# Two-layer decoder trunk: x given with its features on partitions, 1/rms applied where the projections are evicted, layer B's first weights made in the output projection's last chunk

## The chip, the cores and the metric

One NeuronCore of a Trainium2 chip. The time is the device time of one execution in microseconds (us), the median of several runs. TensorE is PE (its weight loads PEld), VectorE DVE, ScalarE ACT, GpSimd POOL; SP issues nearly all DMAs, in the order of its own queue.

## The reference

Two decoder layers over x of 2048 tokens (S) and 1024 features (D), in fp32. Cut to what matters here:

```python
def rmsnorm(x, g):
    return x * rsqrt(mean(x * x, -1) + EPS) * g
# layer A: 16 heads of 64
u = rmsnorm(x, norm_a_g)
q, k, v, f, gate = split(u @ w_in_a)
q, k = rmsnorm(q, qnorm_a_g), rmsnorm(k, knorm_a_g)          # per head
o = causal_attention(q, k, v, bias=cumsum(log_sigmoid(f + b_forget)))
h = x + (o * silu(gate)) @ w_out_a
# keys and values of layer B, and layer B
k_s, v_s = split(rmsnorm(h, kv_norm_g) @ w_kv)                # k: norm, rope
q, gate = split(rmsnorm(h, norm_b_g) @ w_in_b)                # q: norm, rope
o = sliding_window_attention(q, k_s, v_s, sinks)
out = h + (o * silu(gate)) @ w_out_b
```

## The kernel before

Every fp32 operand of a large matmul is kept as two fp32r parts, high and low, and a product is three matmuls (high by high, high by low, low by high). A projection of 128 tokens onto 512 columns takes 8 pieces of 128 features, so 24 matmuls of 512 columns. "Block" is 128 tokens (16 of them, NTB), "chunk" 512 tokens (4, CH).

The stages in order of time, with lines of the kernel before:

- **Layer A's projections**, 12 to 604 us, `projections` (matmul L586): seven groups of columns, each over 16 blocks; the first is a group of v heads. In the first group `normer.upto` loads a block of x with tokens on partitions (L308, into tiles st and wr in turn), takes its squares' sum on ACT (L310), its 1/rms with small DVE operations and one ACT square root (L296 to L301), multiplies the block by it (DVE L314), turns it with eight PE transposes into a PSUM buffer b2 (L287), and splits that into the high part (ACT L323) and the low part (DVE L324). These parts (tiles big) stay for the other groups, and are written out for the gate.
- **Attention of layer A**, 605 to 1473 us: scores L803 and L804, values L844, running sums L829. The gate projection (L875; 32 tiles of 128 features by 512 tokens, 24 matmuls each, one PSUM buffer pb) is fed in between, matmul by matmul, by `feed`; 28 tiles fall into this stage. A finished gate tile goes through ACT (Tanh, L882) and DVE (L883).
- **Output projection of layer A**, 1500 to 1683 us, `out_a` (L1071): per chunk eight tiles of 128 tokens by 512 columns. Each loads its part of x into a buffer qn (L1061), adds it to PSUM (L1075) and stores h from the same buffer (L1076). Beside a chunk the gated inputs of the next are made (`gated`, L1027 to L1031, loads into st and wr). In the last chunk, which has no next one, layer B's norm of the first blocks runs: loads of h, transposes, splits.
- **Layer B's projections**, 1683 to 1990 us, the same `projections`: the first group's weights are w_kv, in four loads of 512 KB through two buffers wr (L349), and each is split into two wh (ACT L366) and two wl (DVE L367).
- **Gate of layer B** to 2180 us (L557, Silu L563), and attention and output projection of layer B to the end.

Order: each engine runs its instructions in one fixed order, which a scheduler makes from the program; buffers come round in turn, so that an operation waits until the last reader of its buffer is done. b2 has three PSUM buffers, shared by projections, transposes and out_a; pa and pb one each. SBUF buffers: wr 2, st 4, qn 3, wh and wl 9 each, big 8.

Of the kernel before, what the change touches and what calls it, by code (L numbers as in the profile page):

```python
# [13 lines left out]
F32R = mybir.dt.float32r  # L14
# [8 lines left out]
P = 128  # L23
# [31 lines left out]

JOBS_AT = (0, 3, 6, 9)
# [17 lines left out]
SLOTS = dict(big=8, st=4, wr=2, wh=9, wl=9, sq=2, qn=3, rot=1, ro1=1, ro2=2)  # L74
# [13 lines left out]
class Trunk:  # L88
# [7 lines left out]
    def __init__(self, ctx, tc, a, out):  # L96
# [4 lines left out]
            for name, shape in (  # L101
# [9 lines left out]
                ("rd", [H, S]),  # L111
                ("h1", [S, D]),
# [176 lines left out]
    def rstd(self, sm, n, count):  # L289
# [5 lines left out]
        ss, v, r, t = (sm[:, i, :n] for i in range(4))  # L295
# [5 lines left out]
        nc.vector.scalar_tensor_tensor(r, t, 1.5, r, ALU.add, ALU.mult)  # L301
        return r

    def norm(self, src, tb, junk):

        nc = self.nc
        xt = self.sb(("st", "wr")[tb % 2], [P, D])
        nc.sync.dma_start(out=xt, in_=src[tb * P : (tb + 1) * P, :])  # L308
        sm = self.sb("sm", [P, 4, 8], bufs=4)
        nc.scalar.activation(  # L310
            junk, xt.rearrange("p (c t) -> p c t", t=P), AF.Square, accum_out=sm[:, 0, :1]
        )
        r = self.rstd(sm, 1, D)
        nc.vector.tensor_scalar(xt, xt, r, None, ALU.mult)  # L314
        return xt

    def norm_transpose(self, xt, uh, ul):

        nc = self.nc
        ps = self.ps("b2", [P, NDT, P])  # L320
        for dt in range(NDT):
            self.flip(ps[:, dt, :], xt[:, dt * P : (dt + 1) * P])
        nc.scalar.copy(uh, ps)  # L323
        nc.vector.tensor_tensor(ul, ps, f_(uh), ALU.subtract)  # L324
# [49 lines left out]
    def qk_norm(self, ps, nh, tb, rope):  # L374
# [4 lines left out]
        nc.scalar.activation(sq, pv, AF.Square)  # L379
        sm = self.sb("sm", [P, 4, 8], bufs=4)  # L380
        nc.vector.tensor_reduce(sm[:, 0, :nh], sq, AX.X, ALU.add)  # L381
        r = self.rstd(sm, nh, HD)
        qn = self.sb("qn", [P, nh, HD])
# [36 lines left out]
    def v_tile(self, ps, nh, dst):  # L420
        nc = self.nc
        st = self.sb("sq" if nh <= 4 else "st", [P, nh, P])
        pv = ps.rearrange("p (h d) -> p h d", d=HD)
        nc.scalar.copy(r_(st[:, :, :HD]), pv)
        nc.vector.tensor_tensor(r_(st[:, :, HD:]), pv, st[:, :, :HD], ALU.subtract)  # L425
        nc.sync.dma_start(out=dst, in_=st)

# [10 lines left out]
    def normer(self, src):  # L438

        uh, ul, ready = {}, {}, []  # L440
# [8 lines left out]

        def upto(n, loads=()):  # L450

            while done[1] < min(n, NTB):
                while done[0] < min(done[1] + LOADED_AHEAD, NTB):
                    _, junk = parts(done[0])
# [920 lines left out]
```

## Time and profile before

| | |
|---|---|
| median of 3 runs | 2541.59 us (2537.08 to 2541.75) |
| the profiled execution | 2537.57 us, its span 2535.7 us |
| mean granted TensorE clock | 0.996 |
| TensorE busy | 2477.2 us (98% of the span) |
| VectorE, ScalarE, GpSimd busy | 67%, 53%, 37% |

The profile is of one execution; all times inside it are from its span's start. TensorE's idle time is short and scattered, but for the start, the end of the attention and the join of the layers near 1684 us.

### The profile page before, as it was taken

What the parts mean: (1) busy time and instruction counts of PE and PEld (TensorE: products, weight loads), DVE (VectorE), ACT (ScalarE), POOL (GpSimd) and SP (SyncE); (2) the same over time, 40 slices, a digit from 0 to 9 for tenths busy, and PEclk for the clock granted to TensorE, in tenths of its full rate; (3) what the DMA queues carried; (4) which work ended last, traced back from release to release, by engine and by line L of the source; (5) the groups of instructions that cost most, each with busy time, mean ns of one, the idle gap of its engine ahead of it and who ended that gap; (6) DMA issues with size and microseconds to landing.
All of it is one profiled execution on the core that took longest, in us unless ns stands there. A gap on an engine that the chain in (4) does not pass through costs nothing.

```text
span 2535.7 us, 37563 instructions
## 1 busy us (share of the span) xinstructions
PE 2477.2 (98%) x12414; PEld 2065.3 (81%) x12414; DVE 1693.9 (67%) x4158; ACT 1335.0 (53%) x2614; POOL 941.3 (37%) x611
## 2 busy tenths in 40 slices
PE   8999999999999999999999999989999999899999
PEld 7888899987878787877887778767888888788887
DVE  5555556636888888888888964437666301788885
ACT  5423323314777787877787731124332213777774
POOL 0000000013777777877788832200011000355552
PEclk9999999999999999999999999999999999999999
DMA  5656555686545655565456678935434424756651
GB/s 185 181 153 188 163 148 170 186 272 207 158 143 138 188 159 151 158 180 151 126 152 200 178 232 264 274 127 150 125 108 109 143 82 127 196 156 162 169 143 66
DMA packets 355217, 416.13 MB, mean 164 GB/s; under 512 B 65072, under 2 KB 248368, under 8 KB 348848
## 3 DMA queue, kind: packets, MB, share of 16 engines
q1 hardware_dynamic: 355024, 413.75, 56.5%
q8 instruction: 98, 1.61, 0.3%
q14 instruction: 95, 0.78, 0.1%
HBM read 262.13 MB, written 151.39 MB: 163 GB/s over the span
## 4 chain that ended last, share of the span: by engine, by line
PE 84%; DMA 7%; DVE 4%; ACT 2%; issue 2%; SPq 1%; POOL 1%; DVEq 0%; ACTq 0%; POOLq 0%
PE b L586 30%; PE pa L844 9%; PE b L557 7%; PE pb L1217 6%; PE pb L875 6%; PE sc L803 5%; PE mx L755 5%; PE sc L804 5%; PE b L287 3%; DMA wr<-rd 3%; PE b L1071 2%; PE pa L1182 2%; PE b L1126 1%; PE b L1123 1%; PE pb L287 1%
## 5 line engine op out<-in xcount | busy, mean ns | idle before, releaser
L586 PE MATMUL b<-wh,big 128*128 128x512 f32 (+3 forms) x2560 | 774.3, 376 | 11.7 <-ACT wh L366 7.9
L818 POOL TENSOR_TENSOR big<-st,big 128x1024 fp32r<-128x1024 f32 (+1 forms) x320 | 680.6, 2140 | 243.1 <-ACT big L817 163.7
L586 PEld LDWEIGHTS b<-wh,big 128*128 128x128 f32 x2560 | 473.4, 189 | 83.4 <-ACT wh L366 10.4
L586 PE MATMUL b<-wl,big 128*128 128x512 f32 (+3 forms) x1280 | 475.8, 372 | 0.3 <-DVE wl L367 0.3
L829 DVE TENSOR_TENSOR ac<-ac,st 128x512 f32<-128x512 f32 (+3 forms) x576 | 355.0, 616 | 60.4 <-ACT ac L821 23.1
L844 PE MATMUL pa<-big 128*128 128x512 f32 (+2 forms) x1280 | 332.6, 373 | 3.0 <-POOL big L818 2.0
L812 ACT ACTIVATE st<-sc 128x512 f32<-128x512 f32 (+1 forms) x512 | 275.3, 584 | 103.5 <-PE sc L804 67.8
L817 ACT CAST big<-st 128x1024 fp32r<-128x1024 f32 (+1 forms) x320 | 302.2, 944 | 9.4 <-PE pa L844 1.2
L586 PEld LDWEIGHTS b<-wl,big 128*128 128x128 f32 x1280 | 242.8, 190 | 37.4 <-DVE wl L367 4.2
L844 PEld LDWEIGHTS pa<-big 128*128 128x128 f32 x1280 | 225.5, 190 | 43.6 <-ACT sq L852 7.4
L803 PE MATMUL sc<-big 128*128 128x512 f32 (+2 forms) x640 | 245.8, 384 | 1.4 <-DVE st L425 1.4
L766 DVE CUSTOM_DVE_ANT_0 mx<-mx,rot 128x128 f32<-128x128 f32 (+3 forms) x240 | 211.0, 879 | 44.7 <-PE mx L755 42.0
L804 PE MATMUL sc<-big 67*128 67x512 f32 (+2 forms) x640 | 236.2, 369 | 0.0
L379 ACT ACTIVATE sq<-b 128x512 f32<-128x512 f32 (+2 forms) x128 | 66.3, 518 | 322.2 <-PE b L586 321.1
L755 PE MATMUL mx<-big 66*128 66x128 f32 (+3 forms) x660 | 190.1, 361 | 2.6 <-DVE mt L766 1.5
L381 DVE TENSOR_REDUCE sm<-sq 128x8 f32<-128x512 f32 (+2 forms) x128 | 74.9, 585 | 162.0 <-ACT sq L379 161.6
L1071 PE MATMUL b<-big 128*128 128x512 f32 x768 | 177.6, 391 | 2.9 <-DVE qn L1075 1.8
L875 PE MATMUL pb<-wh,wr 128*128 128x512 f32 x448 | 166.2, 401 | 7.1 <-DMA wr<-wg 5.2
L1071 PEld LDWEIGHTS b<-big 128*128 128x128 f32 x768 | 143.1, 188 | 36.0 <-DVE qn L1075 3.9
L681 POOL MEMSET rot<- 128x1024 bf16 x1 | 1.0, 951 | 430.6 <-PE pb L287 430.6
L557 PE MATMUL b<-big,wh 128*128 128x512 f32 x512 | 158.7, 391 | 1.5 <-ACT st L563 1.5
L1152 POOL TENSOR_TENSOR st<-st,rs 128x1024 f32<-128x1024 f32 (+1 forms) x64 | 118.7, 1855 | 102.0 <-DVE rs L1151 87.8
(222 smaller groups left out, 4207.7 us busy)
## 6 DMA issues: line engine op xcount, KB each, us to landing
wr<-wg SPq DMA_DIRECT2D x60, 512.0 KB, 5.3
va<-st SPq DMA_DIRECT2D x32, 512.0 KB, 3.6
ka<-st SPq DMA_DIRECT2D x64, 256.0 KB, 3.8
ut<-big SPq DMA_DIRECT2D x16, 1024.0 KB, 5.5
big<-ka SPq DMA_DIRECT2D x16, 1024.0 KB, 6.5
big<-qa SPq DMA_DIRECT2D x16, 1024.0 KB, 5.0
qb<-st SPq DMA_DIRECT2D x64, 256.0 KB, 3.8
big<-qb SPq DMA_DIRECT2D x16, 1024.0 KB, 6.4
```

What stands on the lines that cost most here:

```text
L557: nc.tensor.matmul(ps, W[k][dt][:, ft * P : (ft + 1) * P], u[ch][:, dt, :], start=(dt == 0 and i == 0), stop=(dt == NDT - 1 and i == 2),)
L586: nc.tensor.matmul(ps[:, :n], u[tb // 4][:, dt, us], W[k][dt], start=(dt == 0 and i == 0), stop=(dt == NDT - 1 and i == 2),)
L755: mm = nc.tensor.matmul(ps[:, b, :wb], qb[:66, i * P : (i + 1) * P], kb[:66, k0 + b * wb : k0 + (b + 1) * wb], start=True, stop=True,)
L803: nc.tensor.matmul(o, ka[:, ks], qa[:, qs], start=not (last and n_), stop=False)
L804: nc.tensor.matmul(o, kb[:, ks], qb[:, qs], start=False, stop=not diag)
L812: nc.scalar.activation(pf[:, off : off + w], ps[:, :w], AF.Exp, scale=HD**-0.5)
L817: nc.scalar.copy(ph[:, :tw], pf[:, :tw])
L818: nc.gpsimd.tensor_tensor(pl[:, :tw], pf[:, :tw], f_(ph[:, :tw]), ALU.subtract)
L829: nc.vector.tensor_tensor(a_, a_, pf[:, off : off + w], ALU.add)
L844: nc.tensor.matmul(pv[:, q0 : q0 + w], v[:, k, :], src[:, off : off + w], start=(p == 0 and n_ == 0 and i == 0), stop=(last and n_ == 1 an ...
L875: nc.tensor.matmul(ps, w[:, dt // 2 % 2, wk, dt % 2, :], us[dt][uk], start=(dt == 0 and i == 0), stop=(dt == NDT - 1 and i == 2),)
L1071: nc.tensor.matmul(ps, y[p // 4][:, k, p % 4, ts_], W[nh][j][p], start=(p == 0 and i == 0), stop=(p == NDT - 1 and i == 2),)
```

## The change

- **x_t.** The host also hands in x as (block, feature in piece, piece, token). Layer A loads its blocks from it (`load_block`), already turned, and splits them straight from SBUF (`split_block`); transposes and the multiply by 1/rms are gone there. For 1/rms the block is squared in place (ACT), summed over its eight pieces (DVE, `block_squares`), and then over partitions with one plain fp32 matmul by a column of ones (`block_sums`), which stands after piece 4 of the block's projection in the first group. 1/rms goes into a column `factors`. At the very start the loads stand as x block 0, the weight vector, the four loads of weights, and then x blocks 1 and 2; before, block 1 went ahead of the weights.
- **1/rms at evictions**, in both layers: as the scale of the ACT operations that read the projections' PSUM (Square in `qk_norm`, copy in `v_tile`), as a scalar in DVE operations (v's low part, the forget logits), and as one more DVE operation on 128x8 numbers in `qk_norm`. Layer B's blocks of h are still turned by PE, but no longer multiplied before. Features of a gate lie on partitions, so the gates need 1/rms as a row: `rstd_row` turns the column and stores it (rr), `factor_rows` loads 512 of its numbers to all partitions (tile rows, one buffer), and every gate tile has a DVE multiply of PSUM by rows ahead of its Tanh or Silu. In layer A the second factor of silu is put into the reciprocals of the softmax sums.
- **rest.** After a finished gate tile, `feed` skips once.
- **w_kv early.** The first weights of layer B are made at the start of `out_a`'s last chunk (`given = last()`).
- **Buffers.** qn has two buffers instead of three; rows takes the place of the third. Layer B's v blocks go round over qn, qn and rows.

```diff
-SLOTS = dict(big=8, st=4, wr=2, wh=9, wl=9, sq=2, qn=3, rot=1, ro1=1, ro2=2)
+SLOTS = dict(big=8, st=4, wr=2, wh=9, wl=9, sq=2, qn=2, rows=1, rot=1, ro1=1, ro2=2)
...
+    def load_block(self, src, tb):
         xt = self.sb(("st", "wr")[tb % 2], [P, D])
-        nc.sync.dma_start(out=xt, in_=src[tb * P : (tb + 1) * P, :])
+        if len(src.shape) == 4:
+            self.nc.sync.dma_start(out=xt.rearrange("p (c t) -> p c t", t=P), in_=src[tb])
+        else:
+            self.nc.sync.dma_start(out=xt, in_=src[tb * P : (tb + 1) * P, :])
+        return xt
+    def split_block(self, xt, turned, uh, ul):
+        if turned:
+            u = xt.rearrange("p (c t) -> p c t", t=P)
+        else:
+            u = self.ps("b2", [P, NDT, P])
+            for dt in range(NDT):
+                self.flip(u[:, dt, :], xt[:, dt * P : (dt + 1) * P])
+        nc.scalar.copy(uh, u)
+        nc.vector.tensor_tensor(ul, u, f_(uh), ALU.subtract)
+    def block_squares(self, xt):
+        nc.scalar.activation(xt, xt, AF.Square)
+        sums = self.sb("ro2", [P, P])
+        nc.vector.tensor_reduce(sums, xt.rearrange("p (c t) -> p t c", t=P), AX.X, ALU.add)
+        return sums
+    def block_sums(self, sums, tb):
+        ps = self.ps(("pa", "pb")[tb % 2], [P, 1])
+        self.tc.keep_in_program_order(
+            nc.tensor.matmul(ps, sums, self.ones[:, :1], start=True, stop=True)
         )
...
-        nc.vector.tensor_scalar(xt, xt, r, None, ALU.mult)
-        return xt
...
+    def rstd_row(self, r, i):
+        ps = self.ps("pa", [NTB, P])
+        self.tc.keep_in_program_order(self.flip(ps, r))
+        row = self.sb("ro1", [NTB, P])
+        nc.vector.tensor_copy(row, ps)
+        nc.sync.dma_start(out=self.d["rr"][i].rearrange("(b t) -> b t", t=P), in_=row)
...
+        nc.scalar.activation(sq, pv, AF.Square, scale=r0)
...
+        nc.vector.tensor_scalar(r, r, r0, None, ALU.mult)
...
-        nc.vector.tensor_tensor(r_(st[:, :, HD:]), pv, st[:, :, :HD], ALU.subtract)
+        nc.scalar.activation(r_(st[:, :, :HD]), pv, AF.Copy, scale=r0)
+        nc.vector.scalar_tensor_tensor(
+            r_(st[:, :, HD:]), pv, r0, st[:, :, :HD], ALU.mult, ALU.subtract
...
                 while done[0] < min(done[1] + LOADED_AHEAD, NTB):
-                    _, junk = parts(done[0])
-                    ready.append(self.norm(src, done[0], junk))
+                    load(done[0])
-                    if done[0] > 1:
-                        for load in loads:
-                            load()
-                        loads = ()
-                self.norm_transpose(ready.pop(0), *parts(done[1]))
+                    for other in loads:
+                        other()
+                    loads = ()
...
+        def factor(tb, dt):
+            if turned and dt == 0:
+                blocks[tb] = self.block_squares(blocks[tb])
+            if turned and dt == FACTOR_AT:
+                sm = self.sb("sm", [P, 4, 8], bufs=3)
+                rstd(tb, sm, self.block_sums(blocks.pop(tb), tb))
...
+            if gi or first is None:
+                W = self.weights(
+                    grp["w"], grp["c0"], grp["n"], grp["gain"], x2, ahead=None if gi else raw0
+                )
+            else:
+                W = first
...
                         sg = self.sb("st", [P, CH])
-                        nc.scalar.activation(sg, ps, AF.Silu)
+                        nc.vector.tensor_tensor(sg, ps, rows, ALU.mult)
+                        nc.scalar.activation(sg, sg, AF.Silu)
...
             late = []
             for tb in range(NTB):
                 norm(tb + NORM_AHEAD)
+                if gi == 1 and tb == ROW_AT:
+                    self.rstd_row(factors, row)
+                r0 = factors[:, tb : tb + 1]
...
                         hook(tb, dt)
+                    if gi == 0:
+                        factor(tb, dt)
...
             nc.vector.reciprocal(rc, ps)
+            nc.vector.tensor_tensor(rc, rc, factors[:nr, 1 if c0 else 0], ALU.mult)
...
-                us = []
+                rows, us = self.factor_rows(0, ch), []
...
                     g = self.sb("sq", [P, CH])
-                    nc.scalar.activation(g, ps, AF.Tanh, scale=0.5)
+                    nc.vector.tensor_tensor(g, ps, rows, ALU.mult)
+                    nc.scalar.activation(g, g, AF.Tanh, scale=0.5)
                     nc.vector.scalar_tensor_tensor(g, g, 1.0, ps, ALU.add, ALU.mult)
...
         def feed(n, pause=False):
+            nonlocal fed, rest
+            if pause and rest:
+                rest = False
+                return
             while fed < min(total, n):
                 next(filler, None)
                 fed += 1
                 if pause and fed % (3 * NDT) == 0:
+                    rest = True
                     break
...
+            if not more:
+                given = last()
```

The order of instructions moves at three places. On PE, in the first group of layer A (wh and wl are weights, big the parts of x, b2 PSUM): before, the end of the first block, the transposes of a later one, and the second block;

```order
L586 MATMUL b2_228<-wh_202,big_123 128x512
L586 MATMUL b2_228<-wl_203,big_123 128x512
L586 MATMUL b2_228<-wh_202,big_124 128x512
L287 MATMUL b2_270<-ident_85,st_152 128x128 x8
L586 MATMUL b2_281<-wh_174,big_123 128x512
L586 MATMUL b2_281<-wl_175,big_123 128x512
```

after, inside the first block (the projection's matmul is now L663):

```order
L663 MATMUL b2_176<-wl_157,big_136 128x512
L663 MATMUL b2_176<-wh_156,big_137 128x512
L343 MATMUL pa_196<-ones_82,ro2_178 128x1
L663 MATMUL b2_176<-wh_160,big_136 128x512
L663 MATMUL b2_176<-wl_161,big_136 128x512
```

The eight transposes between blocks are gone, and one matmul by ones stands inside each.

On DVE, at the end of `out_a`: before, the last adds of x (L1075), the low parts of h (L324), and then the low parts of w_kv;

```order
L1075 TENSOR_TENSOR qn_16243<-b2_16245,qn_16243 128x512
L324 TENSOR_TENSOR big_16089<-b2_16285,big_16088 128x8x128
L1075 TENSOR_TENSOR qn_16296<-b2_16298,qn_16296 128x512
L1075 TENSOR_TENSOR qn_16325<-b2_16327,qn_16325 128x512
L324 TENSOR_TENSOR big_16089<-b2_16365,big_16088 128x8x128
L367 SCALAR_TENSOR_TENSOR wl_16379<-wr_16376,g_kv_115,wh_16378 128x512
L367 SCALAR_TENSOR_TENSOR wl_16383<-wr_16376,g_kv_115,wh_16382 128x512
L367 SCALAR_TENSOR_TENSOR wl_16389<-wr_16386,g_kv_115,wh_16388 128x512
L367 SCALAR_TENSOR_TENSOR wl_16393<-wr_16386,g_kv_115,wh_16392 128x512
```

after, in the last chunk, up to the adds of its first two tiles (L1175; L301 to L307 make a 1/rms, L397 is the low part of weights):

```order
L397 SCALAR_TENSOR_TENSOR wl_16099<-wr_16092,g_kv_116,wh_16098 128x512
L301 TENSOR_SCALAR sm_16184<-sm_16184 128x1
L303 RECIPROCAL sm_16184<-sm_16184 128x1
L304 TENSOR_TENSOR sm_16184<-sm_16184 128x1
L305 SCALAR_TENSOR_TENSOR sm_16184<-sm_16184 128x1
L307 SCALAR_TENSOR_TENSOR r_15064<-sm_16184 128x1
L397 SCALAR_TENSOR_TENSOR wl_16105<-wr_16102,g_kv_116,wh_16104 128x512
L397 SCALAR_TENSOR_TENSOR wl_16109<-wr_16102,g_kv_116,wh_16108 128x512
L397 SCALAR_TENSOR_TENSOR wl_16115<-wr_16112,g_kv_116,wh_16114 128x512
L397 SCALAR_TENSOR_TENSOR wl_16119<-wr_16112,g_kv_116,wh_16118 128x512
L1175 TENSOR_TENSOR qn_16122<-b2_16124,qn_16122 128x512
L1175 TENSOR_TENSOR qn_16151<-b2_16153,qn_16151 128x512
```

All low parts of w_kv now stand ahead of the last chunk's first add.

On SP, with the waits: before, the last stores of h and then w_kv;

```order
L1076 DMA h1_67<-qn_16243 128x512 [waits DMAHW0_49,DVE_49]
L1076 DMA h1_67<-qn_16296 128x512 [waits DVE_49]
L1076 DMA h1_67<-qn_16325 128x512 [waits DMAHW2_49,DVE_49]
L349 DMA wr_16376<-in_w_kv 128x2x512 [waits PE_49,Activation_49]
L349 DMA wr_16386<-in_w_kv 128x2x512 [waits DMAHW4_49,DMAHW3_49,DVE_49]
L349 DMA wr_16396<-in_w_kv 128x2x512 [waits DMAHW5_49,DMAHW4_49,DVE_49]
L349 DMA wr_16406<-in_w_kv 128x2x512 [waits DMAHW5_49,DVE_49]
```

after, between the loads of x for the last two tiles of chunk 2 (qn_16053 is the last) and those for the first two of chunk 3 (qn_16122, qn_16151; L1161 loads x, L1176 stores h, L315 loads h, L379 the weights):

```order
L379 DMA wr_16082<-in_w_kv 128x2x512 [waits DMAHW1_49]
L1161 DMA qn_16053<-in_x 128x512 [waits DMAHW7_49,DMAHW2_49]
L379 DMA wr_16092<-in_w_kv 128x2x512 [waits DMAHW5_49,DMAHW4_49,DMAHW6_49,DMAHW3_49,DVE_49]
L1176 DMA h1_68<-qn_16019 128x512 [waits DVE_49]
L315 DMA st_16180<-h1_68 128x1024 [waits Activation_49,Pool_49]
L1176 DMA h1_68<-qn_16053 128x512 [waits DVE_49]
L379 DMA wr_16102<-in_w_kv 128x2x512 [waits DMAHW1_49,DVE_49]
L379 DMA wr_16112<-in_w_kv 128x2x512 [waits DMAHW3_49,DMAHW0_49,DVE_49]
L1161 DMA qn_16122<-in_x 128x512 [waits DMAHW4_49]
L1161 DMA qn_16151<-in_x 128x512 [waits DMAHW6_49,DMAHW2_49]
```

The loads of w_kv now stand among them, two of them behind DVE's low parts of the first two.

## Rows read from the trace of the kernel before

**Rows 1.** Page, part 1: busy us of each engine, share, instructions.

```profile
PE 2477.2 (98%) x12414; PEld 2065.3 (81%) x12414; DVE 1693.9 (67%) x4158; ACT 1335.0 (53%) x2614; POOL 941.3 (37%) x611
```

**Rows 2.** Stretches: length, busy of PE, PEld, DVE, ACT, POOL; clock; DMA share, GB/s.

```profile
20.20:114.00 93.80, 93.80 (x472) 78.89 (x471) 46.74 (x129) 41.80 (x71) 0.00 (x0) 1.00 0.51 149
600.00:1000.00 400.00, 395.47 (x1947) 317.68 (x1946) 334.34 (x617) 312.70 (x489) 309.16 (x148) 1.00 0.59 166
...
1400.00:1480.00 80.00, 74.23 (x336) 57.81 (x336) 72.63 (x107) 59.91 (x97) 65.68 (x32) 0.96 0.58 163
...
1684.00:1725.00 41.00, 29.93 (x119) 22.42 (x120) 17.46 (x50) 13.15 (x26) 1.91 (x6) 0.88 0.32 103
```

**Rows 3.** Timeline of the start: start, duration, engine, line; idle before and its releaser.

```profile
0.81 0.40 SPq L308 DMA_DIRECT2D st<-in_x  x1
...
4.58 1.06 ACT L310 ACTIVATE big<-st 128x1024 fp32r<-128x1024 f32 x1 [2.28 <-DMA st<-in_x]
...
7.87 1.94 PE L287 MATMUL b<-ident,st 128*128 128x128 f32 x8 [7.87 <-DVE sm L296]
...
8.29 2.62 ACT L366 ACTIVATE wh<-big,g_a 128x512 fp32r<-128x512 f32 x4 [0.27 <-DMA big<-in_w_in_a]
...
12.00 0.79 PE L586 MATMUL b<-wh,big 128*128 128x512 f32 x1 [0.39 <-ACT big L323]
...
21.97 1.04 PE L287 MATMUL b<-ident,st 128*128 128x128 f32 x8
```

**Rows 4.** Chain of waits, first group: first and last of 14 blocks.

```profile
23.01 5.47 PE b L586 x24
...
105.43 5.47 PE b L586 x24
```

**Rows 5.** Timeline: the plain fp32 matmul of the softmax sums, and a later one.

```profile
665.38 0.30 PE L726 MATMUL sc<-fold,part 128*64 128x32 f32 x2
...
666.19 0.28 PE L803 MATMUL sc<-big 128*128 128x256 f32 x1
```

**Rows 6.** Timeline of the join of the layers.

```profile
1682.83 1.04 PE L287 MATMUL b<-ident,wr 128*128 128x128 f32 x8
...
1684.16 18.18 SPq L349 DMA_DIRECT2D wr<-in_w_kv  x4
...
1688.23 1.34 ACT L366 ACTIVATE wh<-wr,g_kv 128x512 fp32r<-128x512 f32 x2 [3.32 <-DMA wr<-in_w_kv]
1688.99 1.42 DVE L367 SCALAR_TENSOR_TENSOR wl<-wr,g_kv,wh 128x512 fp32r<-128x512 f32 x2 [2.81 <-ACT wh L366]
...
1689.01 0.80 PE L586 MATMUL b<-wh,big 128*128 128x512 f32 x1 [5.14 <-ACT wh L366]
...
1690.39 1.05 PE L586 MATMUL b<-wh,big 128*128 128x512 f32 x2
...
1692.84 0.63 PE L586 MATMUL b<-wh,big 128*128 128x512 f32 x2
```

**Rows 7.** Timeline of out_a's last chunk.

```profile
1636.38 0.33 SPq L1076 DMA_DIRECT2D h<-qn  x1
...
1647.51 1.04 PE L287 MATMUL b<-ident,st 128*128 128x128 f32 x8
```

**Rows 8.** DMA issues: count, KB, median us from issue to landing.

```profile
qn<-in_x SPq DMA_DIRECT2D x32, 256.0 KB, 4.0
...
h<-qn SPq DMA_DIRECT2D x32, 256.0 KB, 4.6
...
wr<-in_w_kv SPq DMA_DIRECT2D x4, 512.0 KB, 3.5
```

**Rows 9.** Lines by form: busy us, mean ns; idle before, what ended it.

```profile
L557 PE MATMUL b<-big,wh 128*128 128x512 f32 x512 | 158.7, 391 | 1.5 <-ACT st L563 1.5
...
L883 DVE SCALAR_TENSOR_TENSOR sq<-sq,pb 128x512 f32<-128x512 f32 x28 | 18.9, 674 | 0.4 <-ACT sq L882 0.3
...
L1029 DVE TENSOR_TENSOR qn<-qn 128x512 f32<-128x512 f32 x7 | 10.3, 1468 | 4.2 <-DMA qn<-gt 4.1
```

## What the change was predicted to do

> **What bounds the kernel now.** The page's first part comes first: TensorE is busy 98% of the span [rows 1], so nothing is won by making another engine faster; a gain must take work off TensorE or close one of its few gaps. Second, the table by stretches [rows 2] says how near the others are in each stage. In the first projection group TensorE is busy all 93.80 us while VectorE works 46.74 and ScalarE 41.80, half of it. In the attention TensorE has 395.47 of 400 us, but VectorE 334.34 (84%), and in the attention's last 80 us VectorE has 72.63 (91%) while TensorE falls to 74.23. The 41 us after the output projection are the worst stretch: TensorE has 29.93, and its granted clock there is 0.88 in the mean. Third, timelines of the start, of the join and of out_a's last chunk [rows 3, 6, 7] show which wait ends last at each.
>
> **The start.** In the profile before, x's first block is there at 4.58 (its ACT squares start), the weights' first split at 8.29, and the first projection matmul at 12.00, released by the split of the turned block; between them lie the square root chain, the multiply and the transposes at 7.87. The first block is done when the next transposes start, 21.97 [rows 3]. After the change the split of x needs only the load, so it is done before the weights. These come earlier, since x's second block no longer goes ahead of them: 512 KB take 3.5 us by themselves [rows 8], so between 0 and 3.5; I take half, 1.8. The first split of weights is then at 6.5, and at 0.67 each (two in 1.34 [rows 6]) the first matmul can start at about 7.2. This early the matmuls run at the lower level of the clock: two of them take 1.05 after an idle time, and 0.63 later [rows 6], so each loses 0.21 against 0.228 (24 in 5.47 [rows 4]). 24 of them from 7.2 on, all slow, end at 7.2 + 24 x 0.438 = 17.7 instead of 21.97: **-4.3**. If the clock rises before the block ends it is up to -6.5; if x's second block, now behind the weights, comes late, -2.
>
> **The first group.** Fourteen blocks start 6.34 apart ((105.43 - 23.01) / 13), of which the matmuls are 5.47 [rows 4]. The rest, 0.87, is one set of eight transposes. Fourteen such sets lie behind 21.97, as that is where the first of them stands: 14 x 0.87 = **-12.2**. In their place come 16 matmuls by ones, in plain fp32. Nearest is the fp32 sum of the softmax: its record is 0.30, and from its start to the next but two it is 0.81, with two 512-column matmuls (0.46) in between, 0.35 in all [rows 5]. I take 0.30 each, **+4.8**, with 0.22 to 0.45 (3.5 to 7.2) as bounds. The Trainium skill, page "FP8 and Floating Point Precision", section "TensorE Precision Notes", says that true fp32 takes four passes through the array; the row has two records for one such matmul, so this trace does not bear it out, and with twice the records the sum would be 4.8 higher. Two flips of the factor column cost as much as two such sums, **+0.6**. What else is added here (Square in place, a sum of 128x1024 on VectorE, at twice a 512-column split 1.42 [rows 6]) replaces a multiply, a square and a read of PSUM of like size, and is covered by the half of each period in which both engines stand idle [rows 2]. Without that cover it would cost 1.42 a block, 20 us. The small multiply of 128x8 numbers in `qk_norm` lies under the same cover.
>
> **The join.** After out_a the last transposes start at 1682.83, w_kv is only issued at 1684.16, the first matmul starts at 1689.01 after 5.14 idle, and the later pieces come one by one [rows 6]. In all TensorE idles 41.00 - 29.93 = 11.07 us there [rows 2]. With w_kv split long before, these waits go. I leave 0.7 for the handing over from add to store to load of the last blocks of h: **-10.4** (-7, if these become the next to be late, to -12).
>
> **Out_a's last chunk, where the loads went.** The order of DVE and SP, shown with the change, is what I go by. DVE now has all eight low parts of w_kv ahead of the chunk's first add; TensorE may run two tiles and a set of transposes ahead on its three b2 buffers and then needs that add. The second pair of loads of w_kv waits on SP for the low parts of the first, and the second of these stands behind the add of chunk 2's last tile. That tile's x is loaded into one of now only two qn buffers, after the store of the tile two before: issued 1636.38, 4.6 to land, 1641.0; load 4.0, 1645.0; add and low part 0.7 each, 1646.4; third load of w_kv 3.5, 1649.9. The fourth load follows after the low parts of the second, 1647.8, and lands 1651.3; one high part 0.67 and two low parts 1.42 end at 1653.4, and the first add at 1654.1 [rows 6 to 8]. TensorE has its two tiles and the transposes behind it at 1647.51 + 0.87 = 1648.4 [rows 4, 7]. So it waits 5.7, and after the stop runs slow as it did from 1689.01 to 1692.84, where 3.8 us at the lower level lose 1.8 [rows 6]. **+7.5**; 2 if the loads land early, 11 if two waits add up.
>
> The other chunks of out_a with two qn buffers: a buffer is gone for load 4.0, add 0.7 and store 4.6, 9.3 us [rows 8], and must serve every second tile, each 10.9 (twice 24 matmuls [rows 4]). It fits with 1.6 to spare: **+0.5**.
>
> **Layer A's attention.** 28 gate tiles get a multiply of a PSUM tile by an SBUF tile. The nearest row of that shape and those operands is the gate's own L883, 674 ns; with both inputs in SBUF beside GpSimd it can be 1468 [rows 9]. So 28 x 0.67 = 19 us of VectorE, or 41 at most. It has 16% free in the middle, 9% at the end [rows 2]; the single bank of the gate is held longer, and `rest` gives one matmul's place back for that. I take **+2**, for the end of the stage, between -2 (the skip removes the waits on L883) and +8.
>
> **Layer B.** Its gate tiles get the same multiply, but the bank is now freed by DVE before the Silu; TensorE waits 1.5 us in all for that Silu today [rows 9]: **0**, between -1.5 and +2. The multiply taken off its norm lies under TensorE's work.
>
> **Sum.** -4.3 - 12.2 + 4.8 + 0.6 - 10.4 + 7.5 + 0.5 + 2 = -11.5 on the profiled 2537.57, so 2526.1. The median shown is 4.0 above that execution, though one run lies beside it; I add half: **2528**. Its own range, from the bounds of the terms, is 2518 to 2535.
>
> **Rivals.**
> - *No stall in the last chunk.* The loads land early, or the first add is in time, as before the change, when it stood ahead of any weight: -7.5, 2520.5. Against it: two loads in a row, each behind a split.
> - *Two qn buffers are too few.* If SP issues a load or store over 1.6 us late on the mean, the qn cycle and not TensorE sets out_a's pace. At 0.8 us over on each of 16 pairs it gives 12.8 back: 2541, the same as before. For it: gated loads share that queue; against it, three b2 banks.
> - *Slower: VectorE in the attention.* If a gate tile's multiply also stands behind another operation of its size, 0.67 + 0.70 reach TensorE 28 times, 38 us in place of 2: 2564. It decides from 0.75 us per tile (21 us over the forecast). For it: 91% in the end; against it: 16% of VectorE free in the middle, where TensorE's own gaps are 1% [rows 2].
> - *The transposes' time doesn't come free,* as the block's split, squares and sums make ScalarE or VectorE late in the first group: 12.2 back, 2540. Against it: both at half.
> - *The sums take four passes.* 16 x 0.30 more, 2533. Against it: the two records [rows 5].
>
> **How the numbers follow.** A measurement here can tell about 0.2%, 5 us. Chances: the forecast .52, no stall .17, too few qn .12, VectorE .08, the first group .05, four passes .06. The forecast, no stall and four passes lie below 2536.5: faster .76 with the part of the forecast's tail and of the qn case that fall either way; same .16; slower .08. The range leaves out VectorE and the last of each tail: 2516 to 2541.
>
> **What would show it.** In the profile of the changed kernel: a first projection matmul near 7 us; blocks of the first group about 5.8 apart; no transposes there, and records of the ones matmul of about 0.3; a wait of TensorE on DVE's add in out_a's last chunk, some 5 to 6 us, followed by slow matmuls; no wait of TensorE on the split of w_kv; 28 DVE rows of about 0.67 before Tanh. It is wrong if the blocks keep 6.3, if out_a's tiles wait for x in every chunk, or if TensorE's busy share in the attention falls by more than a point.

## The result

The changed kernel takes 2546.6 us, median of 8 runs (2541.6 to 2550.7), beside 2537.6 (2534.6 to 2541.8) for the kernel before in 8 runs: 1.003 of it, 95% interval 1.0017 to 1.0042. It is slower by 9.0 us by the medians, 0.3%; 2528 was forecast, in a range of 2516 to 2541.

Stage by stage, from the first and last matmuls of each in the two profiled executions, in us (the attention ends with the last matmul of its gate; "rest" is from the end of layer B's projections to the end of the span):

| | layer A's projections end | attention A | out_a | layer B's projections, the join in them | rest | span |
|---|---|---|---|---|---|---|
| before | 603.6 | 897.2 | 182.2 | 309.0 | 543.7 | 2535.7 |
| after | 599.3 | 908.4 | 195.1 | 293.7 | 549.9 | 2546.4 |
| difference | -4.3 | +11.2 | +12.9 | -15.3 | +6.2 | +10.7 |
| forecast | -11.1 | +2 | +8 | -10.4 | 0 | -11.5 |

TensorE has no more work than before; it waits more, and its mean granted clock is 0.993 for 0.996. The page's first part and four stretches of the profile after (columns as in [rows 1, 2]):

```profile
PE 2474.7 (97%) x12320; PEld 2058.7 (81%) x12320; DVE 1788.7 (70%) x4353; ACT 1350.7 (53%) x2598; POOL 938.7 (37%) x611
```

```profile
20.20:114.00 93.80, 90.17 (x406) 74.28 (x405) 71.02 (x154) 47.19 (x69) 0.00 (x0) 0.98 0.63 185
600.00:1000.00 400.00, 397.03 (x1953) 318.50 (x1954) 348.24 (x642) 316.70 (x497) 314.40 (x149) 1.00 0.57 164
1400.00:1480.00 80.00, 69.59 (x315) 53.70 (x314) 70.22 (x97) 54.64 (x88) 58.38 (x29) 0.94 0.48 140
1660.00:1703.00 43.00, 37.00 (x164) 30.64 (x165) 15.21 (x44) 12.07 (x23) 0.00 (x0) 0.92 0.47 159
```

In the first group VectorE now has 71.02 of 93.80 us, where 46.74 were [rows 2]; the 3.63 in which TensorE is not busy are one wait at the group's end, shown below. The middle of the attention is as full as before, with VectorE up from 334 to 348. Its end lost: 69.59 of 80 us for TensorE, 74.23 before. The last row is out_a's last chunk: 6 us idle, and a granted clock of 0.92.

**The start and the first group** did nearly what was forecast, up to the group's end:

```profile
8.68 0.79 PE L663 MATMUL b<-wh,big 128*128 128x512 f32 x1 [8.68 <-ACT wh L396]
...
23.36 0.28 PE L343 MATMUL pb<-ones,ro 128*128 128x1 f32 x2
...
28.82 0.28 PE L343 MATMUL pa<-ones,ro 128*128 128x1 f32 x2
...
34.51 0.28 PE L343 MATMUL pb<-ones,ro 128*128 128x1 f32 x2
```

The first matmul starts at 8.68 (7.2 forecast). The sums, one in each block, are 5.69 apart from the third on, where blocks were 6.34 apart [rows 4], so the transposes are gone and a sum costs 5.69 - 5.47 = 0.22. The group ends 11.4 us earlier: at 105.43 + 2 x 5.47 = 116.4 before, and nine matmuls and a sum's 0.22 after the last sum at 102.75, 105.0, now. But some 6 of these 11 us are lost in the next rows, of ScalarE, SP and PE at the end of that group:

```profile
96.65 1.28 ACT L271 ACT_TABLE_LOAD   x1
...
98.38 1.28 ACT L302 ACT_TABLE_LOAD   x1
99.67 0.20 ACT L302 ACTIVATE sm<-sm 128x1 f32<-128x1 f32 x1
...
102.31 0.20 ACT L302 ACTIVATE sm<-sm 128x1 f32<-128x1 f32 x1 [0.89 <-DVE sm L301]
103.41 0.69 ACT L455 ACTIVATE st<-b,r 128x512 fp32r<-128x512 f32 x1 [0.90 <-DVE r L307]
...
104.00 1.94 ACT L396 ACTIVATE wh<-wr,g_a 128x512 fp32r<-128x512 f32 x3
...
105.57 1.70 SPq L379 DMA_DIRECT2D wr<-in_w_in_a  x2
...
110.78 1.33 ACT L396 ACTIVATE wh<-wr,g_a 128x512 fp32r<-128x512 f32 x2 [1.99 <-DMA wr<-in_w_in_a]
...
111.55 0.80 PE L663 MATMUL b<-wh,big 128*128 128x512 f32 x1 [3.63 <-ACT wh L396]
```

Evictions L455 need their block's 1/rms, and the second group's weight splits (L396) stand behind them on ScalarE. The square root of one block, at 99.67, is itself late: it stands behind two loads of ScalarE's function tables, 1.28 us each, of which one is for the sine of the angles (L271). The next block's comes after it, at 102.31, so that block's eviction at 103.41 still waits 0.90 for r, the splits follow at 104.00, and only then the loads into the two wr buffers can be issued, 105.57. They are split at 110.78; PE, which is half through the second group's first block sooner than before, waits 3.63 and then runs at the lower clock level (granted clock 0.50 from 110.5 to 117.3 us).

**Out_a's last chunk** shows the stall as it was derived, 7.51 in place of 5.7:

```profile
1655.03 3.00 SPq L379 DMA_DIRECT2D wr<-in_w_kv  x2
...
1663.93 1.41 DVE L397 SCALAR_TENSOR_TENSOR wl<-wr,g_kv,wh 128x512 fp32r<-128x512 f32 x2 [1.78 <-ACT wh L396]
...
1665.26 1.28 DVE L1175 TENSOR_TENSOR qn<-b,qn 128x512 f32<-128x512 f32 x2
...
1666.00 2.50 PE L1171 MATMUL b<-big 128*128 128x512 f32 x5 [7.51 <-DVE qn L1175]
```

The third and fourth load of w_kv (one row) start at 1655.03, their low parts end on VectorE at 1665.3, the first add follows, and PE after it.

**The end of the attention** was the largest miss of a term. GpSimd, VectorE, ScalarE and PE there:

```profile
1452.17 5.17 POOL L903 TENSOR_TENSOR big<-st,big 128x1024 fp32r<-128x1024 f32 x2
...
1452.24 2.87 DVE L1123 TENSOR_TENSOR qn<-qn,wl 128x512 f32<-128x512 f32 x1 [1.82 <-POOL qn L1122]
...
1455.51 2.39 DVE L1124 TENSOR_TENSOR qn<-qn 128x512 f32<-128x512 f32 x1
...
1458.61 0.72 DVE L801 TRANSPOSE_TENSOR_REDUCE part<-ac 128x16 f32<-128x512 f32 x1
...
1459.36 0.59 ACT L906 COPY ac<-st 128x512 f32<-128x512 f32 x1 [3.05 <-DVE part L801]
...
1460.37 0.58 ACT L937 COPY sq<-pa 128x512 f32<-128x512 f32 x1
...
1461.00 1.22 PE L929 MATMUL pa<-big 128*128 128x512 f32 x2 [3.92 <-ACT sq L937]
```

VectorE's L1123 and L1124 (gated inputs for out_a, prepared here) lie over two instructions of GpSimd, L903, and take 2.87 and 2.39 us. Behind them on VectorE stands the sum L801; ScalarE waits 3.05 for it, its copy of PSUM (L937) is next in its queue, and PE waits 3.92 for the buffer that this copy frees.

### The profile page after: what moved, and what is told of

Its sections match the earlier page's. It is cut to its first block, busy times and chain, and to the rows that moved or that the text cites. A ratio compares the mean times of both kernels' runs of the same rounds, so it can differ in the third digit from the quotient of the medians.

```text
span 2546.4 us, 37588 instructions
## 1 busy us (share of the span) xinstructions
PE 2474.7 (97%) x12320; PEld 2058.7 (81%) x12320; DVE 1788.7 (70%) x4353; ACT 1350.7 (53%) x2598; POOL 938.7 (37%) x611
## 5 line engine op out<-in xcount | busy, mean ns | idle before, releaser
L663 PE MATMUL b<-wh,big 128*128 128x512 f32 (+3 forms) x2560 | 774.3, 376 | 13.2 <-ACT wh L396 12.8
L903 POOL TENSOR_TENSOR big<-st,big 128x1024 fp32r<-128x1024 f32 (+1 forms) x320 | 678.2, 2132 | 254.3 <-ACT big L902 164.6
L663 PEld LDWEIGHTS b<-wh,big 128*128 128x128 f32 x2560 | 473.9, 189 | 84.2 <-ACT wh L396 14.2
L663 PE MATMUL b<-wl,big 128*128 128x512 f32 (+3 forms) x1280 | 475.7, 372 | 1.1 <-DVE wl L397 0.9
L663 PEld LDWEIGHTS b<-wl,big 128*128 128x128 f32 x1280 | 242.6, 190 | 37.4 <-DVE wl L397 4.9
L409 ACT ACTIVATE sq<-b,r 128x512 f32<-128x512 f32 (+2 forms) x128 | 77.8, 608 | 314.5 <-PE b L663 314.4
L840 PE MATMUL mx<-big 66*128 66x128 f32 (+3 forms) x660 | 189.4, 360 | 8.9 <-DVE mt L851 7.1
L1171 PEld LDWEIGHTS b<-big 128*128 128x128 f32 x768 | 145.8, 191 | 46.2 <-DVE qn L1175 10.9
```

Source lines behind the costliest of these rows:

```text
L663: nc.tensor.matmul(ps[:, :n], u[tb // 4][:, dt, us], W[k][dt], start=(dt == 0 and i == 0), stop=(dt == NDT - 1 and i == 2),)
L840: mm = nc.tensor.matmul(ps[:, b, :wb], qb[:66, i * P : (i + 1) * P], kb[:66, k0 + b * wb : k0 + (b + 1) * wb], start=True, stop=True,)
L903: nc.gpsimd.tensor_tensor(pl[:, :tw], pf[:, :tw], f_(ph[:, :tw]), ALU.subtract)
L1171: nc.tensor.matmul(ps, y[p // 4][:, k, p % 4, ts_], W[nh][j][p], start=(p == 0 and i == 0), stop=(p == NDT - 1 and i == 2),)
```

## Experiments

Each is the changed kernel with one edit unless said otherwise. In the table the ratio is to the kernel before on the same chip, with its 95% interval; stages as above, from one profile each. What one profile can tell is seen where nothing differs: layer A's projections are the same in nine of these kernels (the changed one, e1, e2, e4 to e6, e11 to e13) and end at 596.9 to 599.4; layer A's attention is the same in the changed kernel, e1, e2, e3 and e11 and takes 907.5 to 913.1. In e4, e6, e12, e13 and e14 out_a's first matmul comes 1.4 to 2.2 us after the gate's last, waiting for that gate tile on VectorE; this is counted in out_a.

| run | median us | ratio | A's projections end | attention A | out_a | B's projections | rest |
|---|---|---|---|---|---|---|---|
| e1 w_kv late | 2556.2 | 1.0079 (1.0066 to 1.0091) | 598.8 | 910.7 | 186.2 | 313.6 | 548.8 |
| e2 w_kv after tile 2 | 2538.6 | 1.0013 (1.0004 to 1.0023) | 596.9 | 909.9 | 188.2 | 293.6 | 548.9 |
| e3 sums earlier | 2542.8 | 1.0029 (1.0018 to 1.0041) | 595.9 | 907.5 | 191.7 | 293.1 | 549.0 |
| e4 no multiply, A | 2532.0 | 0.9992 (0.9983 to 1.0001) | 598.3 | 898.8 | 191.3 | 293.4 | 552.3 |
| e5 three qn | 2576.7 | 1.0163 (1.0143 to 1.0182) | 597.4 | 897.2 | 190.5 | 293.2 | 596.6 |
| e6 no skip | 2533.5 | 0.9995 (0.9981 to 1.0008) | 597.8 | 899.5 | 189.8 | 293.1 | 549.6 |
| e7 x as before | 2569.5 | 1.0136 (1.0114 to 1.0159) | 609.9 | 913.3 | 188.5 | 297.7 | 553.9 |
| e8 before, w_kv early | 2530.6 | 0.9984 (0.9972 to 0.9997) | 601.6 | 897.1 | 195.0 | 292.7 | 543.9 |
| e10 layer A as before | 2549.2 | 1.0042 (1.0026 to 1.0058) | 613.0 | 896.2 | 189.4 | 297.8 | 552.3 |
| e11 no multiply, B | 2543.8 | 1.0022 (1.0009 to 1.0034) | 599.4 | 913.1 | 195.8 | 295.0 | 546.1 |
| e12 e2 and e6 | 2529.6 | 0.9969 (0.9958 to 0.998) | 598.3 | 901.9 | 185.3 | 293.3 | 551.5 |
| e13 e4 and e6 | 2533.4 | 0.999 (0.9979 to 1.0001) | 597.5 | 897.0 | 190.1 | 293.1 | 550.7 |
| e14 e2, e3 and e6 | 2524.6 | 0.9953 (0.994 to 0.9967) | 596.0 | 896.7 | 186.7 | 293.3 | 549.7 |

**e1, w_kv late.** `given = last()` is taken out, so layer B makes its first weights itself.

> w_kv is made after the output projection again, all else as in the changed kernel. Theory (the split of w_kv ahead of the first add makes the 7.51 us wait in the last chunk): that wait goes, to under 1 us, and the join's 11 us of waits come back; out_a gets 9 us shorter, the join 12 to 15 longer, the total 2 to 5 us longer than the changed kernel's 2546.6. Rival (two qn buffers are themselves too few for out_a): a wait of 4 us or more on the add stays in the last chunk, and the total is 8 us or more longer.

```profile
1660.83 9.40 PE L1169 MATMUL b<-big 128*128 128x512 f32 x40 [1.70 <-DVE qn L1173]
...
1701.31 0.80 PE L663 MATMUL b<-wh,big 128*128 128x512 f32 x1 [4.80 <-ACT wh L396]
```

The 7.51 is gone, but waits on the add of 1.75, 1.44 and 1.70 stand in three chunks: out_a is 4 us longer than before the change without any w_kv in it, so the rival holds in part. The join costs more than expected: early weights are worth 19.9 us there (313.6 to 293.7) for 8.9 in out_a. The whole, 1.0079 for the changed kernel's 1.003, is longer by 12 us, where the theory had 2 to 5 and the rival 8 or more.

**e2, w_kv after the last chunk's second tile.**

```diff
-            if not more:
-                given = last()
...
+                    if not more and nh == 0 and tb == 1:
+                        given = last()
                     if ch == NCH - 1 and tb % 2:
                         norm(2 * nh + tb // 2 + 1)
```

> w_kv is made after the second tile of the last chunk in place of ahead of the first, so that the first two adds stand ahead of its last four low parts on VectorE. Theory (order on VectorE): the wait of 7.51 us falls under 1.5 us, with the slow matmuls behind it; 7 to 9 us less than the changed kernel, 2538 to 2540. Rival (the loads of w_kv crowd out x's loads, or two qn buffers are too few): 5 us or more of wait stay.

The wait in the last chunk falls to 2.26, out_a gets 6.9 shorter, the join keeps its gain: order on VectorE, as the theory has it, and the 2 us left are of the kind that e1 shows.

**e3, sums one block earlier.**

```diff
-                        factor(tb, dt)
+                        for b in {0: (0,), 1: (1, 2)}.get(tb, (tb + 1,)):
+                            if b < NTB:
+                                factor(b, dt)
```

> The squares, sums and 1/rms of a block are made one block earlier in the first group (from block 2 on). Theory (evictions that wait for 1/rms stand ahead of the next group's weight splits on ScalarE and make their loads late): the wait of 3.63 us between the first two groups falls under 1 us, the slow matmuls behind it go too; 4 to 6 us less than the changed kernel. Rival (the loads themselves are slow, 5.2 us, since the blocks end earlier than before): the wait stays at 2.5 us or more.

```profile
93.33 0.38 PE L343 MATMUL pa<-ones,ro 128*128 128x1 f32 x2 [1.72 <-DVE ro L335]
...
110.40 0.51 PE L665 MATMUL b<-wh,big 128*128 128x512 f32 x1 [0.67 <-ACT wh L396]
```

The wait between the groups falls from 3.63 to 0.67: evictions that wait for 1/rms made it. A new one comes, of a sum on its VectorE reduction (1.72), so the stage gains 3.4 beside the changed kernel's profile, and 1 to 3.5 beside the range above, not 5. The whole, 1.0029, can't be told from the changed kernel's 1.003.

**e4, no multiply of layer A's gate tiles.** Tanh reads PSUM; 1/rms is missing from that gate, and the loads of rows go with it.

> Layer A's gate tiles are not multiplied by 1/rms (left out, with the load of rows): Tanh reads PSUM as before the change; two qn buffers and the skip stay. Theory (19 us more of VectorE work is what the attention's end pays): PE's waits from 1350 us to the end of the attention fall from some 20 us to under 11, 8 to 12 us less than the changed kernel. Rival (the two qn buffers delay the gated inputs that are prepared there): at most 4 us less, and the waits of 2 us and more there stay.

The attention is 9.6 shorter, though TensorE's idle time behind the 24th gate tile (of the 28 in this stage) falls from 20.6 to 14.8 us, not to under 11. That alone would fit 19 us of VectorE work of which half shows; e5 and e6 say otherwise.

**e5, three qn.** `qn=3`, no tile rows; both gates are multiplied by ones and lack 1/rms.

> Three qn buffers again, room made by leaving out the tile rows: the gate tiles are multiplied by a column of ones instead (same instruction, so 1/rms is missing from both gates). Theory so far (the multiply pays for the attention's end; the two qn buffers for about 4 us of out_a, and the v block that waits for rows for about 4 us of layer B's attention): attention within 3 us of the changed kernel's 908 us, out_a outside the one 7.5 us wait 3 to 5 us shorter, from layer B's gate on 4 to 5 us shorter; 7 to 10 us less than the changed kernel. Rival (the gated inputs that are prepared in the attention lack the third buffer): the attention itself gets 6 us or more shorter, the total 13 or more.

The rival: with multiply and skip in place, the attention is 11.2 shorter, as before the change. The run leaves out the loads of rows as well, like e4, so it doesn't test the third buffer by itself; e6 keeps them. The last stage is 47 us longer; in layer B's attention TensorE now waits 34 times for ScalarE, 16.0 us, and 15 times for VectorE, 13.2. Why, I did not follow, and it doesn't bear on the attention of layer A.

**e6, no skip.** `rest = True` is taken out.

> The skip of one feed after a finished gate tile is taken out, all else as changed. Theory (the longer chain from the gate's PSUM tile to its release makes the next gate matmul wait, which the skip hides): 28 waits of PE on the gate's last DVE operation come back in small pieces, the attention gets 3 to 12 us longer. Rival (the skip shifts gate matmuls to the end, where VectorE is full): the attention gets 2 us or more shorter.

The rival again: 8.9 shorter, with multiply and two buffers in place.

**e7, x as before.** `self.normer(x)` in place of `self.normer(a["x_t"])`.

> Layer A's blocks come from x with tokens on partitions again and are turned by PE; 1/rms still goes in at the evictions, and the rest of the change stays. Theory (x_t is worth 12 us of transposes less the sums, minus the 5 us that the late weights of the second group cost): the projections of layer A get 2 to 8 us longer, the start included, and the stages behind them keep their lengths; 2 to 8 us more than the changed kernel. Rival (the loads of x_t, 8.4 us to land where x took 4.0, and the sums eat all of it): within 2 us of the changed kernel.

Missed: 10.6 longer in the projections and other sizes everywhere. Here and in e10 (below) TensorE has hardly a wait in layer A's projections (none of 0.3 us here, one of 1.26 in e10), but its matmuls of 512 columns take 2% longer, so the run says nothing of x_t's worth.

**e8, the kernel before with early weights** (the edit of e2 and what hands the weights on).

> The kernel before, with only this of the change: w_kv made in the last chunk, after its second tile; layer A, the gates and three qn buffers as before. Theory (the join is the one part of the change that pays, and the last chunk costs nothing if the adds keep their place): PE's idle time of 11 us between out_a and the first blocks of layer B falls under 2, out_a keeps its 182 us within 2; 9 to 13 us less than the kernel before, 0.995 to 0.9965. Rival (the loads of w_kv take the place of x's and h's loads whatever the order): out_a 4 us or more longer, and the gain under 6 us.

```profile
1653.43 1.41 DVE L367 SCALAR_TENSOR_TENSOR wl<-wr,g_kv,wh 128x512 fp32r<-128x512 f32 x2
...
1654.76 0.74 DVE L314 TENSOR_SCALAR st<-st,sm 128x1024 f32<-128x1024 f32 x1
...
1655.56 1.97 PE L287 MATMUL b<-ident,st 128*128 128x128 f32 x8 [9.77 <-DVE st L314]
```

The join gains 16, out_a loses 13. The rival's size, by a mechanism that neither had: in the kernel before, TensorE's transposes of h need VectorE's multiply L314, which now stands behind w_kv's low parts. The change reads h unmultiplied, and that takes this wait away; e10 shows what is left without the multiply.

**e9, the three mends** of e2, e3 and e6 together; a first run.

> Three mends of the changed kernel together: no skip of a feed, w_kv made after the last chunk's second tile, sums one block earlier. Theory (they stand at places that don't touch each other, so what each was worth alone adds up: 9 in the attention, 7 in out_a, 3 in the first group): about 19 us less than the changed kernel, 0.995 to 0.997 of the kernel before. Rival (each build gets its own order at the attention's end, so the 9 us there need not come again): the attention is at 907 us or more again, and the whole within 10 us of the changed kernel.

It measured 2526.7, 0.9953 (0.9936 to 0.9971), 19 to 20 us less than the changed kernel, as the theory has it. Its stages are read from e14.

**e10, layer A as before**, layer B as changed with e2's edit, three qn, rows in one of them.

> Layer A and its gates wholly as in the kernel before, with three qn buffers; layer B as changed (h turned as it is, 1/rms at its evictions and gates), w_kv made after the last chunk's second tile, rows taken from qn. Theory (what pays is h without a multiply and the early weights; what costs is layer A's): attention 897, out_a 183 to 188 with no wait over 3 us, layer B's first projections 293; 8 to 16 us less than the kernel before, 0.994 to 0.997. Rival (out_a's last chunk waits for h's loads or its splits, as with the kernel before and early weights, 9.8 us): out_a at 192 or more, and within 0.2% of the kernel before.

Missed: it is 0.4% slower than the kernel before, where 0.3 to 0.6% less were expected. Out_a at 189.4 waits 4.72 for a load of h, so neither theory nor rival has it. Layer A's projections end 9.4 us later than before the change, and the last stage is 8.6 longer. In layer A, whose instructions are those of the kernel before, the transposes are 6.45 apart, not 6.34.

```profile
100.21 1.03 PE L291 MATMUL b<-ident,st 128*128 128x128 f32 x8
...
106.66 1.03 PE L291 MATMUL b<-ident,wr 128*128 128x128 f32 x8
```

**e11, no multiply of layer B's gate tiles** (1/rms is missing from that gate).

> Layer B's gate tiles are not multiplied by 1/rms (left out, with its loads of rows): Silu reads PSUM as before; all else as changed. Theory (the last gate tile's chain, one DVE operation longer and waiting in DVE's queue, holds its store and with it SP's queue of loads for layer B's attention): from the end of layer B's first projections to the end of the span 4 to 6 us less than the changed kernel's 549.9. Rival (the v blocks that go through rows, or the order of the attention): within 2 us of it.

```profile
2003.20:2549.30 546.10, 530.31 (x2805) 449.37 (x2803) 320.40 (x1100) 309.31 (x847) 180.83 (x148) 1.00 0.47 139
```

The stage is 546.1 long, 3.8 less than in the changed kernel and 2.4 over the kernel before. In the changed kernel the last gate tile's Silu, store and the load of the output weights behind it in SP's queue come so:

```profile
2187.35 0.63 ACT L635 ACTIVATE st<-st 128x512 f32<-128x512 f32 x1
...
2188.01 0.33 SPq L637 DMA_DIRECT2D gtb<-st  x1
...
2189.73 0.45 SPq L379 DMA_DIRECT2D wr<-in_w_out_b  x1
```

That store is 5.6 us after layer B's gates end, 2.0 before the change and in e11. So the multiply is shown to cost some 4 of the 6 us in this profile, just under the 4 to 6 expected (the whole, 1.0022, can't be told from 1.003). That the cost runs through SP's queue is not shown: in this stage of the changed kernel TensorE's listed waits are for no load, and 2.0 us of them are for the multiply itself, L634.

**e12, no skip and e2.**

> No skip of a feed and w_kv after the last chunk's second tile, sums as changed. Theory (sizes add up): 3 us more than the run with the earlier sums as well, about 16 less than the changed kernel. Rival (the earlier sums are worth nothing, since their own wait of PE took back the other): equal to that run within 1 us.

0.9969 beside 0.9953 with the earlier sums: 2529.6 for 2526.7 us, the 3 us of the theory, but the two intervals overlap, so the worth of the sums is not shown.

**e13, no multiply in A and no skip.**

> Layer A's gate multiply left out (so 1/rms is missing from its gate) and the skip of a feed as well. Theory (one event at the attention's end, which needs multiply, skip and two qn buffers together): the attention is at 897 to 901 us, as with either of the two undone alone, and the whole within 3 us of those runs. Rival (two costs of their own, 9.6 and 8.9 us): the attention is at 888 to 893.

897.0, and 0.999 for the whole beside 0.9992 and 0.9995: the two edits together give no more than either. That is so too if each can only give back what the change took: 897 is also the length before the change.

**e14, the three mends, for their profile.**

> The three mends together once more (no skip, w_kv after the second tile, earlier sums), for their profile. Theory (they add up by stage): layer A's projections end at 595 to 597, the attention takes 899 to 902, out_a 185 to 188, layer B's first projections 293, the rest 549 to 552; 0.995 to 0.997 of the kernel before. Rival: the attention at 907 or more, the gain from elsewhere.

They add up, with the attention 2 us shorter than expected, and this version beats the kernel before by 0.5% and the changed one by 0.8%. The attention's end, from the end of the 24th gate tile to the gate's last matmul, of the kernel before, the changed one and e14 (columns as in [rows 2]):

```profile
1341.60:1500.80 159.20, 147.73 (x681) 115.51 (x680) 134.45 (x209) 109.88 (x175) 113.68 (x55) 0.98 0.64 187
```

```profile
1336.40:1507.70 171.30, 150.66 (x682) 117.35 (x681) 143.45 (x220) 109.21 (x175) 111.19 (x55) 0.95 0.60 175
```

```profile
1327.30:1492.70 165.40, 147.98 (x680) 116.47 (x678) 141.37 (x221) 109.96 (x175) 111.49 (x55) 0.97 0.61 180
```

TensorE's idle time is 11.5 us before, 20.6 in the changed kernel and 17.4 in e14, and its clock is at the higher level for less of the stretch than before (0.95, 0.97 for 0.98). In the changed kernel the three largest waits of PE on other engines there were these (waited for: us in total, times, longest):

```profile
PE mx L840 <- DVE mt L851: 7.1, 4, 2.5
PE pa L929 <- ACT sq L937: 3.9, 1, 3.9
PE sc L888 <- ACT st L897: 1.7, 2, 1.1
```

In e14 the first is 2.0 and the second 0.3, but in the second's place PE waits 5.2 us for GpSimd's L903 (now L905), 0.4 in the changed kernel; in e4 this is 5.0, in e6 5.6:

```profile
PE pa L931 <- POOL big L905: 5.2, 3, 3.4
```

## Why the prediction was wrong

By stages the profiled execution is 22.2 us over the forecast: 6.8 in layer A's projections, 9.2 in the attention, 4.9 in out_a and 6.2 in the last stage, less 4.9 at the join.

**Right, with their sizes.** The transposes: 12.2 of 12.2. The last chunk: the order on VectorE that was read off makes the stall, 7.51 for 5.7, and e2 moves it away. A sum costs 0.22, the lower bound, and not 0.30. That out_a and the join together came out at the -2.4 that was forecast is luck: each part was 4.9 larger than its term. The Trainium skill's four passes ("FP8 and Floating Point Precision", "TensorE Precision Notes") would, by the rival's estimate, have made a sum 0.60; the trace shows two records here too.

**The step that failed first: "+2, for the end of the stage".** The term measured 11.2, outside its own bounds of -2 to +8. The multiply was priced right (671 ns for 0.67) and costs nothing in the middle: the 24th gate tile ends 737.1 us into the stage, 738.0 before. The whole loss lies behind that tile, 171.3 us for 159.2, so the end is not a matter of 9% free time. In e4, e5 and e6 the multiply, the two buffers or the skip is undone, and each gives back 9 to 11 us, two of them no more than one (e13). But only a part of that, 4 to 9 us, comes from the end:

| us | before | changed | e4 | e5 | e6 | e13 | e14 |
|---|---|---|---|---|---|---|---|
| to the end of the 24th gate tile | 738.0 | 737.1 | 732.5 | 733.2 | 732.4 | 734.4 | 731.3 |
| from there to the stage's end | 159.2 | 171.3 | 166.2 | 164.0 | 167.2 | 162.6 | 165.4 |

The change, e1, e2, e3 and e11, whose attention is the same, lie at 737.1 to 740.9 and at 169.5 to 172.2. So each edit also gains where the change had lost nothing, and leaves 3 to 8 us of the end's loss.

What makes the end late is not shown. It looked as if gated inputs came late for want of a qn buffer, and VectorE then met GpSimd. The two lines of VectorE, in the whole of the changed kernel:

```profile
L1123 DVE TENSOR_TENSOR qn<-qn,wl 128x512 f32<-128x512 f32 x7 | 15.8, 2258 | 10.2 <-POOL qn L1122 8.7 <-DMA wl<-rd 1.5
L1124 DVE TENSOR_TENSOR qn<-qn 128x512 f32<-128x512 f32 x7 | 9.1, 1294 | 0.3 <-DMA qn<-gt 0.3
```

L1123 was L1028 before, and L1124 was L1029 [rows 9]:

```profile
L1028 DVE TENSOR_TENSOR qn<-qn,wl 128x512 f32<-128x512 f32 x7 | 8.9, 1278 | 2.2 <-POOL qn L1027 1.5 <-DMA wl<-rd 0.7
```

Together they take 24.9 us for 19.2. But they take 25.0 in e4 and 24.9 in e6, where the attention is 9 us shorter. In e6 the same meeting stands before a wait of PE nearly as long as the 3.92 above (L1122 is the changed kernel's L1123):

```profile
1451.37 5.13 POOL L903 TENSOR_TENSOR big<-st,big 128x1024 fp32r<-128x1024 f32 x2
1451.45 2.81 DVE L1122 TENSOR_TENSOR qn<-qn,wl 128x512 f32<-128x512 f32 x1 [1.02 <-POOL qn L1121]
...
1453.77 1.65 PE L929 MATMUL pa<-big 128*128 128x512 f32 x3 [3.74 <-POOL big L903]
```

Likewise GpSimd's waits for loads into qn, ahead of its part of the gated inputs, are 15.2 us in the changed kernel, 15.6 and 16.8 in e4 and e6, and none before and in e5: the want of a third buffer is real, but e4 and e6 are short with it. The Trainium skill, "SBUF — State Buffer", "SBUF: two separate sides", has VectorE with two SBUF inputs and GpSimd, where it reads SBUF, exclude one another for a whole instruction; the rows agree, as far as L1123 and L1124 are this long where they lie over GpSimd's L903. So the meeting is there, and it is not what the three edits undo; how each moves the order was not followed.

**The second: the first group was costed to its own end.** "Covered by the half of each period in which both engines stand idle" holds inside the group, but I left out who is queued behind an eviction that now waits for 1/rms: the next group's weights. Some 6 of 11 us went there: 3.63 of wait and the slow matmuls behind it, and with earlier sums (e3) the wait is 0.67. The sum of 128x1024 was priced at 1.42 and takes 2.0:

```profile
L335 DVE TENSOR_REDUCE ro<-st 128x128 f32<-128x1024 f32 x8 | 16.0, 1997 | 1.3 <-ACT st L333 1.3
```

**The third: layer B's gates at 0.** The last stage is 6.2 longer, and without the multiply 2.4 (e11). The term let DVE free the bank early; TensorE waits 2.0 us for that very multiply. The rest, and the way of the cost, are open.

**The fourth: two qn buffers at +0.5.** Out_a is 4.0 longer without any w_kv in it (e1). The slack of 1.6 us of 10.9 took loads and stores to be issued at once; in e1 SP waits 13 times, 19.0 us, for a store of h, ahead of a load of x that needs its buffer, 6 times and 11.8 us before, 3 times and 6.0 with three buffers (e5).

The start gave 2 of 4.3: the first split of weights came at 7.90, not 6.5. One profile can't tell this: in e8, whose start is that of the kernel before, the row of 21.97 in [rows 3] stands at 19.84. Of the rivals, "two qn are too few" and "VectorE in the attention" each came in part.

## What to carry to other kernels

Where an eviction starts to need a value that is made late, look at what stands behind that eviction on its engine, at the stage's end above all. Prefetched weights are worth their place only where their splits don't stand ahead of something that frees PSUM: the same loads cost out_a 8.9 or 2 us by their place, and 13 in the kernel before, where TensorE needed one more operation behind the splits. At the end of a stage in which an in-order engine is nine tenths busy, a small edit is not priced by its duration; try it at several places or orders. Before a wait is called the cause, look for it in the run that is faster: here one as long stood in its place.

## What was not expected of the hardware

Two builds (e7, e10) run layer A's matmuls of 512 columns 2% slower at the same granted clock, 1.00, with PE busy throughout: 6.45 us for a block of 24 matmuls and eight transposes in e10, 6.34 before. I did not follow what differs between the builds; the cause is open.
